# Score tiles in the outputs' PSUM banks, and three weight units split on VectorE, in a GLA and conformer step

## Chip, cores and metric

The kernel runs on one core of a Trainium2 chip, with float32 inputs and outputs. The metric is the device time of one execution in microseconds (us), taken as the median of several runs.

## The reference

One step of a two-layer streaming encoder. 512 new frames of one stream ("prompt") and 64 frames of a running one ("sample") pass through a gated-linear-attention (GLA) mixer and a conformer convolution mixer, each with a normalization ahead and a residual add. The change lies in the GLA mixer, whose core for one head is this:

```python
qe = qc * jnp.exp(b)                     # b: running sum of log decay
ke = kc * jnp.exp(-b)
att = jnp.where(mask, qe @ ke.T, 0.0)    # scores, causal
o = att @ vc + qe @ S                    # outputs; S is the state
S = jnp.exp(b_last) * S + (kc * jnp.exp(b_last - b)).T @ vc
...
o = o * lax.rsqrt(jnp.mean(o * o, axis=-1, keepdims=True) + EPS)
y = (o * g_norm * jax.nn.silu(r)) @ w_out
```

There are 4 heads with 256 key and 512 value features each. q, k, v and the gate r are columns of one projection `h @ w_in` with 2048 input features.

## The kernel before, in words

Activations lie feature-major: 128 features on the partitions, all 576 tokens as columns, and a PSUM bank takes half of them (288). Float32 precision comes from splitting each operand in a high and a low part; a projection is then three matmuls, high by high (L224), low activations by high weights (L227), high activations by low weights (L230).

Weights arrive in *units* of 8 blocks of 128 by 128 (512 KB). For a plain unit (`to_unit`, L118 to L131) SyncE's queue loads the raw values (L116, two buffers), ACT rounds them to the high part (L124), and the low part is made in one of two ways. Either DVE subtracts the high part from the raw values (L126), or, for units listed in `dma_lo`, ACT writes the negated raw values in the low part's format (L128) and a transfer issued by POOL adds the weights to it from DRAM (L129). The parts have four buffers.

The heads' stage (from L771) treats four heads, one after the other, with projection blocks of 128 columns laid between as *tiles* (`tile(i)`: two units, 96 matmuls, except the last, which holds three blocks). For each head:

- `decay(h)`: POOL issues loads of two small operands (a L775, w L776), TensorE multiplies them (pz L783), DVE and ACT turn the result into decays (L785 to L819, with scans at L795). `scores(h)` loads q and k from DRAM (ld L767) and scales them (L825).
- `attention(h)`: five score tiles `pa` (L847 to L860). Each has a product on the diagonal (L849), the first three also products with rescaled queries qs (L855, L859). `psum_split` copies each tile to a high part on ACT (athi L725) and a low part on DVE (atlo L726), and POOL masks them (L828). Then ACT scales the keys (kd L874) and TensorE transposes them (ptkd L732, pukd L735).
- `output(h)`: four output tiles po (L894) copied by ACT (o L896), and four small ones for the sample tokens pq (L899, L902) copied by DVE (o L903). Their squares are summed (L607, L610, L611).
- `states(h)`: the new states pS (L925), copied by ACT (so L933) or combined by DVE (s L928), and stored (sp L934, ss L930). `output(h)` loads the old sample state (s L885).
- `norm(h)`: the sums of squares are split (sso L465, L466), summed across partitions by TensorE (m_o L461), and turned into a factor on ACT and DVE (t_o L483, v_o L484, rs L485 to L488), which multiplies the outputs (L911).
- `gates(h)`, called inside the next head: the loaded gate multiplies the outputs (L943, on POOL for the first three heads), and they are spilled to DRAM (L945). The outputs have one buffer, so the next head's copy L896 waits for the last spill.

`values(h)` loads v by transfers that POOL issues (L959, L960). Results of the projection blocks are stored at L973.

PSUM has eight banks. Four belong to the projection (`ps`). Two carry the tag "ms": pz, the score tiles pa, the transposes, pq, pS and the norm's sums m_o take them in turn. Two carry the tag "main": the outputs po, and tiles of a later stage.

The order on each engine is set by a scheduler that simulates a time line, within the dependences and the program's order; `tile(2h + 2)` is bound to come behind the head's first score product, `tile(2h + 3)` behind its last transpose. An edit to a tag or a list so changes the order in places that the edit does not name.

Of the kernel before, what the change touches and what calls it, by code (L numbers as in the profile page):

```python
# [11 lines left out]
F32 = mybir.dt.float32  # L12
# [5 lines left out]
P = 128  # L18
# [31 lines left out]
def emit(nc, tc, x, wg, wa1, wa2, wgo, wc, wco, par, s0, y, sp_out, ss_out, cv_out):  # L50
# [30 lines left out]
    def psum_pool(key, name, bufs):  # L81
        psum[key] = tc.tile_pool(name=name, bufs=bufs, space=PSUM)
        return psum[key].__enter__()
# [6 lines left out]
    px = psum_pool("e", "pse", 1)  # L90
# [13 lines left out]
    def tmp(name, w=T, dt=F32):  # L104
        return s2.tile([P, w], dt, tag="s2", name=name)
# [3 lines left out]
    dma_lo = set()  # L109
# [158 lines left out]
    def plan(groups, srcf):  # L268
        for g in groups:
            for half in range(2):  # L270
                for b in g:
                    chunks.append(lambda i, w=srcf(b), half=half: plain_chunk(i, w, half))
# [241 lines left out]
    base_p = len(chunks)  # L514
    for i, (b, _) in enumerate(gla_pairs):
        plan_full(wg[b], wg[b + 1], ("ra", "rb")[i % 2])
    base_l = len(chunks)
    plan(gla_last, lambda b: wg[b])
    base_o = len(chunks)
# [3 lines left out]
    base_c = len(chunks)  # L523
    plan(conv_groups, lambda b: wc[b])
    base_co = len(chunks)
    dma_lo.update(range(4, base_p), range(base_l, base_o), range(base_c + 4, base_co))
    plan([[0, 1]], lambda f: wco[f])
    for f in range(2, 14, 2):
        plan_pair(wco[f], wco[f + 1])
# [194 lines left out]
    def psum_split(hi, lo, ps):  # L724
        nc.scalar.activation(hi, ps, AF.Copy)  # L725
        nc.vector.tensor_tensor(lo, ps, hi.bitcast(F32), ALU.subtract)  # L726

    def to_tok(src, dst, sample, name):

        pt = px.tile([P, 512], F32, tag="ms", bufs=2, name=f"pt{name}")  # L730
        for i in range(4):
            ins = nc.tensor.transpose(pt[:, i * P : (i + 1) * P], src[:, i * P : (i + 1) * P], ident).ins  # L732
        psum_split(dst[0], dst[1], pt.rearrange("p (i c) -> p i c", i=4))
        pt = px.tile([P, 512], F32, tag="ms", bufs=2, name=f"pu{name}")
        nc.tensor.transpose(pt[:TS, :P], src[:, TP:T], ident)  # L735
        psum_split(sample[0], sample[1], pt[:TS, :P])
        return ins
# [89 lines left out]
    def causal(ap, n):  # L827
        nc.gpsimd.affine_select(out=ap, in_=ap, compare_op=ALU.is_ge, fill=0.0, base=0,  # L828
                                pattern=[[1, n]], channel_multiplier=-1)
# [7 lines left out]
    def attention(h):  # L837

        d = hd[h]
        q, k = d["eq"], d["ek"]  # L840
        att = [gp.tile([P, 1344], F32R, tag=f"at{n}", name=f"at{n}{h}") for n in ("hi", "lo")]
        eo = 0
        first = None
        for i in range(5):
            n = TP - i * P if i < 4 else TS
            w = min(n, P)
            pa = px.tile([P, 512], F32, tag="ms", bufs=2, name=f"pa{h}_{i}")  # L847
            for dt in range(2):
                ins = nc.tensor.matmul(pa[:w, :w], k[:, dt, i * P : i * P + w], q[:, dt, i * P : i * P + w],  # L849
                                 start=(dt == 0), stop=(dt == 1)).ins  # L850
                first = first or ins
            if i < 3:
                for dt in range(2):
                    qs = tmp(f"qs{h}_{i}{dt}")
                    nc.vector.tensor_tensor(  # L855
                        qs[:, : n - P].rearrange("p (j t) -> p j t", t=P),
                        q[:, dt, (i + 1) * P : TP].rearrange("p (j t) -> p j t", t=P),
                        d["ee"][:, dt, eo : eo + 3 - i].unsqueeze(2).broadcast_to([P, 3 - i, P]), ALU.mult)
                    nc.tensor.matmul(pa[:, P:n], k[:, dt, i * P : (i + 1) * P], qs[:, : n - P],  # L859
                                     start=(dt == 0), stop=(dt == 1))  # L860
                eo += 3 - i
            o = OFFS[i]
            psum_split(att[0][:w, o : o + n], att[1][:w, o : o + n], pa[:w, :n])
            for t in att:
                causal(t[:w, o : o + w], w)
        d["qs"] = gp.tile([P, 2, TS], F32, tag="qs", name=f"qsm{h}")
        nc.vector.tensor_copy(d["qs"], q[:, :, TP:])
        d["att"] = att
        kd = [gp.tile([P, 5, DKH], F32R, tag=f"kd{n}", name=f"kd{n}{h}") for n in ("hi", "lo")]
        for dt in range(2):  # L870
            kt = tmp(f"kd{h}{dt}")
            for i in range(5):
                n = P if i < 4 else TS
                nc.scalar.activation(kt[:, i * P : i * P + n], k[:, dt, i * P : i * P + n], AF.Copy,  # L874
                                     scale=d["km"][:, dt, i : i + 1])
            js = slice(dt * P, (dt + 1) * P)
            ins = to_tok(kt, [t[:, :4, js] for t in kd], [t[:TS, 4, js] for t in kd], f"kd{h}{dt}")
        d["kd"] = kd
        return first, ins
# [104 lines left out]
    for h in range(H):  # L984
        scored, turned = attention(h)
        if h:
            gates(h - 1)
        if h < 3:
            start_head(h + 1)
        if h == 0:  # L990
            tile(1)
        tile(2 * h + 2, scored)
        output(h)
        if h < 3:
            scores(h + 1)
        states(h)
        norm(h)
        if h < 3:
            tile(2 * h + 3, turned)
            values(h + 1)  # L1000
# [271 lines left out]
def build():  # L1272
    nc = _bacc.Bacc("TRN2", target_bir_lowering=False, num_devices=1)

    def inp(name, shape):
        return nc.dram_tensor(name, shape, F32, kind="ExternalInput").ap()

    def out(name, shape):
        return nc.dram_tensor(name, shape, F32, kind="ExternalOutput").ap()

    args = [
        inp("x", [P, KT, T]),
        inp("wg", [48, P, KT, P]),
        inp("wa1", [P, KT, RANK]),
        inp("wa2", [96, 1024]),
        inp("wgo", [16, P, KT, P]),
        inp("wc", [48, P, KT, P]),
        inp("wco", [16, P, KT, P]),
        inp("par", [P, PC_N]),
        inp("s0", [P, 8, DVH]),  # L1290
        out("y", [P, KT, T]),
        out("sp", [P, 8, DVH]),
        out("ss", [P, 8, DVH]),
        out("cv", [P, 16, 2 * PAD]),
    ]
    with TileContext(nc, schedule_with_timeline_sim=True) as tc:
        emit(nc, tc, *args)
    return nc
# [47 lines left out]
```

## Time and profile before

| | us |
|---|---|
| median of 3 runs | 1771.37 (1769.4 to 1772.29) |
| the profiled execution | 1776.21 |
| its span in the trace | 1774.5 |

The mean granted TensorE clock of the profiled execution was 0.985 of full speed. The heads' stage lies at about 440 to 740 us of its span.

A row of a waits view tells the engine, what it computes and the line, behind the arrow what ended the wait, then the total in us, how often and the longest. Rows of a timeline tell the start, the duration, the engine, line and operation, output and inputs, their sizes and the count, and in brackets the idle time ahead and its end. PE is TensorE, PEld its weight load, DVE VectorE, ACT ScalarE, POOL GpSimd and SP SyncE.

### The profile page before, as it was taken

To read this page: it belongs to the slowest core of one execution; us is meant where nothing else is said; L and a number is where in the kernel's file an instruction comes from. 1 tells how busy PE (TensorE), PEld (TensorE's weight loads), DVE (VectorE), ACT (ScalarE), POOL (GpSimd) and SP (SyncE) were. 2 spreads that over 40 slices of the span, in tenths; PEclk is the share of its full clock that TensorE was granted. 3 is DMA by queue.
4 is the path that set the end of the run, shared out by engine and by line. 5 is a ranking of instruction groups with operands and counts; after the bars stand their busy time and mean duration, and the time that the engine had idled before them with its cause. 6 is when DMAs were issued, how large, how long until landed. Compare 5 with 4: busy or idle time off the path is not lost.

```text
span 1774.5 us, 31017 instructions
## 1 busy us (share of the span) xinstructions
PE 1722.7 (97%) x12606; PEld 1695.9 (96%) x12606; DVE 1126.0 (63%) x1622; ACT 906.9 (51%) x1229; POOL 491.8 (28%) x455
## 2 busy tenths in 40 slices
PE   8999999999999989999999999999999989999996
PEld 8999999999888878999999999999999989999995
DVE  7677777766344551845566889878888751185554
ACT  7653343345656563623246556565566574353433
POOL 3100000000222313022223455545555442133221
PEclk9999999999999999999999999999999999999998
DMA  7963455434966864643336777877778768623323
GB/s 236 246 154 120 135 148 149 135 122 132 271 178 195 252 188 140 214 135 128 129 130 164 165 163 166 169 162 164 165 160 180 171 151 171 149 74 118 111 89 133
DMA packets 108896, 282.15 MB, mean 159 GB/s; under 512 B 10672, under 2 KB 37168, under 8 KB 107728
## 3 DMA queue, kind: packets, MB, share of 16 engines
q1 hardware_dynamic: 87632, 202.33, 37.9%
q0 software_dynamic: 21120, 77.83, 22.3%
q8 instruction: 99, 1.62, 0.4%
q14 instruction: 45, 0.37, 0.1%
HBM read 242.68 MB, written 37.45 MB: 158 GB/s over the span
## 4 chain that ended last, share of the span: by engine, by line
PE 81%; DVE 6%; DMA 6%; ACT 3%; issue 2%; POOL 1%; SPq 0%; ACTq 0%; DVEq 0%; POOLq 0%
PE ps L230 14%; PE ps L224 14%; PE ps L227 14%; PE d L391 14%; PE c L337 9%; PE c L328 6%; PE db L391 2%; DMA wlo<-wg 2%; PE po L894 1%; DMA spill<-o 1%; PE cb L328 1%; DVE c L1181 1%; PE pS L925 1%; PE pq L337 1%; PE pq L444 1%
## 5 line engine op out<-in xcount | busy, mean ns | idle before, releaser
L124 ACT ACTIVATE whi<-raw 128x1024 fp32r<-128x1024 f32 x296 | 313.5, 1059 | 498.7 <-PE ps L227 160.3
L227 PE MATMUL ps<-h1l,whi 128*128 128x288 f32 x1536 | 330.1, 296 | 0.0
L230 PE MATMUL ps<-h1h,wlo 128*128 128x288 f32 x1536 | 329.7, 296 | 0.0
L224 PE MATMUL ps<-h1h,whi 128*128 128x288 f32 x1536 | 329.6, 296 | 0.0
L1118 DVE SCALAR_TENSOR_TENSOR acc<-ux,pr,acc 128x606 f32<-128x606 f32 x352 | 297.7, 852 | 11.8 <-ACT acc L1108 2.2
L126 DVE TENSOR_TENSOR wlo<-raw,whi 128x1024 fp32r<-128x1024 f32 x168 | 208.4, 1241 | 132.3 <-ACT whi L124 130.1
L224 PEld LDWEIGHTS ps<-h1h,whi 128*128 128x128 f32 x1536 | 248.5, 189 | 0.0
L227 PEld LDWEIGHTS ps<-h1l,whi 128*128 128x128 f32 x1536 | 248.5, 189 | 0.0
L230 PEld LDWEIGHTS ps<-h1h,wlo 128*128 128x128 f32 x1536 | 248.4, 189 | 0.0
L1116 POOL TENSOR_TENSOR sd<-sd,sd 128x606 f32<-128x606 f32 x96 | 153.5, 1599 | 73.4 <-ACT sd L1112 72.2
L129 POOL DMA_DIRECT2D wlo<-wg x36 | 31.8, 882 | 478.7 <-DVE tb L420 335.7
L611 POOL TENSOR_TENSOR ssq<-ssq,sq_x 128x576 f32<-128x576 f32 x35 | 64.0, 1829 | 286.9 <-ACT sq_x L610 281.4
L129 POOL DMA_DIRECT2D wlo<-wc x92 | 80.9, 880 | 218.0 <-ACT wlo L128 170.2
L128 ACT ACTIVATE wlo<-raw 128x1024 fp32r<-128x1024 f32 x128 | 133.6, 1044 | 0.1
L391 PE MATMUL d<-nh,whi 128*128 128x288 f32 x448 | 132.6, 296 | 0.0
L391 PE MATMUL d<-nh,wlo 128*128 128x288 f32 x448 | 131.9, 294 | 0.0
L391 PE MATMUL d<-nl,whi 128*128 128x288 f32 x448 | 131.8, 294 | 0.0
L1112 ACT ACTIVATE sd<-ux,pr 128x606 f32<-128x606 f32 x112 | 87.3, 793 | 55.8 <-POOL sd L1116 55.8
L230 PE MATMUL ps<-nh,wlo 128*128 128x288 f32 x480 | 108.4, 303 | 2.5 <-DMA wlo<-wg 2.5
L227 PE MATMUL ps<-nl,whi 128*128 128x288 f32 x480 | 107.1, 302 | 0.0
L224 PE MATMUL ps<-nh,whi 128*128 128x288 f32 x480 | 106.9, 302 | 0.0
L391 PE MATMUL d<-S,whi 128*128 128x288 f32 x448 | 90.3, 295 | 0.0
(542 smaller groups left out, 3877.8 us busy)
## 6 DMA issues: line engine op xcount, KB each, us to landing
raw<-wc SPq DMA_DIRECT2D x96, 512.0 KB, 4.8
raw<-wg SPq DMA_DIRECT2D x94, 512.0 KB, 4.7
wlo<-wc POOLq DMA_DIRECT2D x92, 512.0 KB, 7.6
wlo<-wg POOLq DMA_DIRECT2D x36, 512.0 KB, 8.6
raw<-wco SPq DMA_DIRECT2D x26, 512.0 KB, 3.8
raw<-wgo SPq DMA_DIRECT2D x25, 512.0 KB, 4.2
ld<-pd SPq DMA_DIRECT2D x29, 288.0 KB, 5.3
vd<-v SPq DMA_DIRECT2D x32, 256.0 KB, 4.6
```

Of the source, the lines that this page charges most:

```text
L124: nc.scalar.activation(hi[:, :w, :], raw, AF.Copy)
L126: nc.vector.tensor_tensor(lo[:, :w, :], raw, hi[:, :w, :].bitcast(F32), ALU.subtract)
L128: nc.scalar.activation(lo, raw, AF.Copy, scale=-1.0)
L129: nc.gpsimd.dma_start(lo, src, accum_op=ALU.add)
L224: nc.tensor.matmul(ps[j], hi[:, kk, :], ah[k][:, j * HT : (j + 1) * HT], start=st, stop=False)
L227: nc.tensor.matmul(ps[j], hi[:, kk, :], al[k][:, j * HT : (j + 1) * HT], start=False, stop=False)
L230: nc.tensor.matmul(ps[j], lo[:, kk, :], ah[k][:, j * HT : (j + 1) * HT], start=False, stop=sp)
L328: nc.tensor.matmul(dst, w[:, o + k, :], v, start=start and k == 0 and i == 0, stop=stop and k == 3 and i == 2, skip_group_check=True)
L337: nc.tensor.matmul(dst[j], w[:, k, :], v[:, j * HT : (j + 1) * HT], start=start[j] and k == 0 and i == 0, stop=stop[j] and k == 7 and i == ...
L391: nc.tensor.matmul(dst, w[:, k, :], v, start=first and k == 0 and i == 0, stop=k == 7 and i == 2, skip_group_check=True)
L1116: nc.gpsimd.tensor_tensor(side, side, t, ALU.add)
L1118: nc.vector.scalar_tensor_tensor(a, v3(u[:, w : w + CW]), cw(w), a, ALU.mult, ALU.add)
```

## The change

Two edits. The score tiles `pa` take their PSUM bank from the tag "main", in turn with the outputs po, and no longer from "ms", where the norm's sums stay. And the first three plain units of the heads' tiles (both of tile 0 and the first of tile 1) leave `dma_lo`, so that DVE makes their low parts by a subtraction (L126) in place of ACT's negated copy (L128) and POOL's adding transfer (L129). The computed values are the same.

```diff
-    dma_lo.update(range(4, base_p), range(base_l, base_o), range(base_c + 4, base_co))
+    dma_lo.update(range(4, base_p), range(base_l + 3, base_o), range(base_c + 4, base_co))
...
-            pa = px.tile([P, 512], F32, tag="ms", bufs=2, name=f"pa{h}_{i}")
+            pa = px.tile([P, 512], F32, tag="main", bufs=2, name=f"pa{h}_{i}")
```

## Prediction

> **What bounds the kernel now.** I read the page first, for what is left to win at all.
>
> ```profile
> span 1774.5 us, 31017 instructions
> PE 1722.7 (97%) x12606; PEld 1695.9 (96%) x12606; DVE 1126.0 (63%) x1622; ACT 906.9 (51%) x1229; POOL 491.8 (28%) x455
> ```
>
> TensorE is busy 97% of the span. An edit that takes no matmul away can win only its idle time, 1774.5 - 1722.7 = 51.8 us, and time in which it ran at a lower clock. The second view is the busy time by stretches of 60 us over the heads (columns: stretch, its us, busy PE, PEld, DVE, ACT, POOL, granted TensorE clock, share of the DMA engines, GB/s).
>
> ```profile
> 440.00:500.00 60.00, 56.14 (x408) 54.11 (x407) 18.36 (x49) 36.81 (x57) 15.02 (x28) 1.00 0.96 260
> 500.00:560.00 60.00, 55.81 (x364) 51.25 (x363) 29.55 (x62) 34.57 (x55) 19.60 (x27) 0.97 0.74 211
> 560.00:620.00 60.00, 55.95 (x348) 50.21 (x347) 30.20 (x64) 38.03 (x60) 19.58 (x27) 0.94 0.72 200
> 620.00:680.00 60.00, 53.32 (x326) 47.18 (x325) 28.93 (x61) 35.86 (x56) 17.47 (x24) 0.94 0.71 203
> ```
>
> The heads are where TensorE is not at its best: 3.9 to 6.7 us of each 60 idle, and a clock of 0.94 in two rows. Nothing else is near its limit, except that the DMA engines are at 0.96 in the first row. The third view is TensorE's waits there, 440 to 740 us (line that waits, what ended the wait, total, times, longest).
>
> ```profile
> PE pa L849 <- DVE v_o L484: 6.0, 3, 4.2
> PE po L894 <- ACT o L896: 4.2, 3, 1.8
> PE ps L230 <- DMA wlo<-wg: 2.5, 2, 1.3
> PE pS L925 <- ACT so L933: 1.8, 2, 1.2
> PE pz L783 <- DMA w<-w2d: 1.2, 1, 1.2
> PE m_o L461 <- ACT sso2h L465: 1.1, 1, 1.1
> PE m_o L461 <- ACT sso1h L465: 1.1, 1, 1.1
> PE pa L849 <- DVE atlo L726: 1.0, 1, 1.0
> PE pS L925 <- DVE o L903: 0.9, 2, 0.4
> PE m_o L461 <- DVE sso1l L466: 0.3, 1, 0.3
> PE m_o L461 <- DVE sso2l L466: 0.3, 1, 0.3
> ```
>
> They sum to 20.4 us. The first row is the one that the change speaks to: a head's first score product needs a bank of the tag "ms", both hold the last norm's sums, and v_o (L484) is their last reader. TensorE's timeline at the longest:
>
> ```profile
> 529.45 0.42 PE L461 MATMUL m_o<-sso0l,onesr 128*128 128x288 f32 x2
> 534.07 1.05 PE L849 MATMUL pa<-eq,c 128*128 128x128 f32 x4 [4.19 <-DVE v_o L484]
> ```
>
> Its price is more than 4.19 us. These are the stretches of the heads at half clock, and under them the 3.4 us ahead of three of them and two stretches that stayed at full clock:
>
> ```profile
> 534.30:537.70 3.40, 3.40 (x16) 3.40 (x16) 3.33 (x8) 1.60 (x2) 0.00 (x0) 0.50 1.10 381
> 592.30:599.10 6.80, 5.98 (x22) 5.53 (x23) 3.04 (x7) 2.64 (x4) 0.46 (x1) 0.50 1.01 299
> 653.80:660.60 6.80, 5.96 (x23) 5.42 (x24) 2.85 (x6) 3.08 (x5) 0.94 (x2) 0.50 1.02 286
> 687.90:694.70 6.80, 6.80 (x25) 6.13 (x24) 0.27 (x2) 1.96 (x3) 1.41 (x1) 0.50 0.07 15
> 588.90:592.30 3.40, 1.89 (x7) 0.94 (x7) 1.51 (x2) 3.34 (x6) 2.62 (x5) 1.00 0.66 156
> 650.40:653.80 3.40, 2.01 (x8) 0.96 (x7) 1.50 (x2) 3.38 (x6) 2.14 (x4) 0.99 0.47 134
> 684.50:687.90 3.40, 1.60 (x11) 1.46 (x12) 0.18 (x1) 1.09 (x2) 0.00 (x0) 1.00 0.98 237
> 619.60:623.00 3.40, 2.60 (x20) 2.37 (x18) 0.94 (x2) 0.00 (x0) 0.00 (x0) 1.00 0.97 250
> 623.00:626.40 3.40, 2.46 (x14) 2.26 (x15) 0.00 (x0) 1.39 (x3) 0.00 (x0) 1.00 0.95 262
> ```
>
> Stretches with TensorE busy 1.6 to 2.0 us of 3.4 were followed by half clock, those with 2.5 to 2.6 were not. Three of the four begin where a head's norm sums and first products wait. At 0.50 a stretch loses half its length: 3.4/2 + 3 x 6.8/2 = 11.9 us. So 20.4 + 11.9 = 32.3 us can be won in the heads, and no more.
>
> [...]
>
> **The change part by part.** *Score tiles in "main".* No instruction is added; the wait of L849 on v_o goes, and with it the reason for the order around it. TensorE's own order at the start of head 1 (ps: projection matmuls, m_o: norm sums of head 0, pa: scores of head 1), before:
>
> ```order
> L230 MATMUL ps_0_1_5648<-nh_1036,wlo_5355 128x288
> L461 MATMUL m_o_5629<-sso0h,onesr 128x288
> L461 MATMUL m_o_5634<-sso0h,onesr 128x288
> L461 MATMUL m_o_5629<-sso0l,onesr 128x288
> L461 MATMUL m_o_5634<-sso0l,onesr 128x288
> L849 MATMUL pa_0_5773<-eq_5187,c_1_5186 128x128 x2
> L224 MATMUL ps_0_0_5930<-nh_957,whi_5409 128x288
> ```
>
> And now:
>
> ```order
> L461 MATMUL m_o_5626<-sso0l,onesr 128x288
> L461 MATMUL m_o_5631<-sso0l,onesr 128x288
> L227 MATMUL ps_0_0_5644<-nl_1012,whi_5351 128x288
> ...
> L230 MATMUL ps_0_1_5645<-nh_1036,wlo_5352 128x288
> L849 MATMUL pa_0_5770<-eq_5184,c_1_5183 128x128 x2
> L859 MATMUL pa_0_5770<-qs_00_5773,c_1_5183 128x384
> ```
>
> Between the last norm sum and the first score 34 projection matmuls now stand, and 9 more among the sums; before there were none, because tile 3's were used up. At 56.14/408 = 0.138 us apiece (first 60 us row) they cover 4.7 us, more than the 4.19. In heads 2 and 3 first score products stand ahead of the last norm sums, with 20 to 40 projection matmuls around them, so the waits of m_o and of pa there have cover too. Gone by this: v_o 6.0, m_o 1.1 + 1.1 + 0.3 + 0.3 = 2.8, atlo 1.0: 9.8 us. Of the pS waits (1.8 + 0.9 = 2.7) I take 1.0, since the pS banks stay in "ms" but no score tile queues for them.
>
> The clock follows: the first three stretches go, 1.7 + 3.4 + 3.4 = 8.5 us. The fourth starts behind the po wait, which has another cause. The chain of waits there:
>
> ```profile
> 617.29 5.77 DMA spill<-o
> ...
> 652.77 12.17 DMA ss<-s
> 665.45 3.37 DMA ld<-pd
> ...
> 677.62 7.85 DMA spill<-o
> 685.64 0.61 ACT o L896
> ```
>
> The outputs have one buffer, so ACT's o (L896) waits for the last head's spill, and po behind it. The score tiles ending sooner do not move that by themselves: what moves it is the earlier gates. I take half of the po wait, 2.1 of 4.2, and half of the fourth stretch, 1.7 of 3.4; the bounds are none and all.
>
> *What the move adds.* po and pa now alternate in two banks: a po must wait for the split (L725, L726) of the fourth and fifth score tile, a score tile of the next head for the last po's copy. The copies of a head's po end before its norm sums can begin, which sum their squares, so the second costs nothing; for the first, the transposes of kd stand between. In head 0 the scheduler uses the freedom otherwise. TensorE's order at head 0's first transposes (ptkd), before:
>
> ```order
> L849 MATMUL pa_4_5137<-eq_4908,c_0_4907 64x64 x2
> L230 MATMUL ps_0_1_5351<-nh_996,wlo_5025 128x288
> L224 MATMUL ps_0_0_5350<-nh_1001,whi_5236 128x288
> L732 MATMUL ptkd_5154<-ident,kd_5148 128x128 x4
> L224 MATMUL ps_0_1_5351<-nh_1001,whi_5236 128x288
> ```
>
> And now:
>
> ```order
> L859 MATMUL pa_1_5101<-qs_11_5107,c_0_4904 128x256
> L230 MATMUL ps_0_1_5230<-nh_1021,wlo_4967 128x288
> ...
> L230 MATMUL ps_0_0_5229<-nh_1031,wlo_4967 128x288
> L732 MATMUL ptkd_5151<-ident,kd_5145 128x128
> L230 MATMUL ps_0_1_5230<-nh_1031,wlo_4967 128x288
> ```
>
> The transposes stand 12 projection matmuls (1.7 us) behind the second score tile, not behind the fifth. They need kd (L874), and ACT does kd behind a unit whose load is late:
>
> ```profile
> 478.75 1.06 ACT L124 ACTIVATE whi<-raw 128x1024 fp32r<-128x1024 f32 x1 [5.25 <-DMA raw<-wg]
> 480.66 1.50 ACT L874 ACTIVATE kd<-c,ke 128x128 f32<-128x128 f32 x5
> ```
>
> If the load is as late as here TensorE stands up to 5.25 us, if it comes sooner not at all; I take the middle, 2.6, and half of one 6.8 us stretch's loss, 1.7. In the last heads the scaled queries (L855) use buffers that the state copies free; a wait of 1.2 us, the longest of the pS row, is put in, between 0 and twice that.
>
> *Low parts on DVE.*
>
> ```profile
> L126 DVE TENSOR_TENSOR wlo<-raw,whi 128x1024 fp32r<-128x1024 f32 x168 | 208.4, 1241 | 132.3 <-ACT whi L124 130.1
> L129 POOL DMA_DIRECT2D wlo<-wg x36 | 31.8, 882 | 478.7 <-DVE tb L420 335.7
> L128 ACT ACTIVATE wlo<-raw 128x1024 fp32r<-128x1024 f32 x128 | 133.6, 1044 | 0.1
> ```
>
> DVE gains 3 x 1.241 = 3.7 us in a stretch where it is busy 18.36 of 60; ACT loses 3 x 1.044 = 3.1 us, POOL's queue 3 x 0.882 = 2.6 us, and three 512 KB loads leave a stretch in which the DMA engines are at 0.96. On the path this ends two waits: ps on wlo 2.5 and, since POOL issues the w load (L776) behind these, pz 1.2. Together 3.7. The cover of DVE's 3.7 us is the projection itself; without it the cost would be 3.7 once.
>
> *The sum.* Gone: 9.8 + 1.0 + 8.5 + 2.1 + 1.7 + 3.7 = 26.8. New: 2.6 + 1.7 + 1.2 = 5.5. Net 21.3 us. Behind the heads TensorE had no idle time that could swallow this:
>
> ```profile
> 760.00:820.00 60.00, 60.00 (x453) 60.00 (x452) 30.38 (x43) 19.59 (x24) 16.57 (x12) 1.00 0.43 144
> ```
>
> With 60.00 of 60 us busy there, a sooner start reaches the end. The profiled execution was 1776.21 us (span 1774.5 and 1.7 outside), so 1754.9; it lies 4.84 us above the median of the runs, 1771.37. Taken from the median: 1750.1. Bounds: with nothing new and all won 32.3, so 1739.1; with the po terms at nothing and the new ones at 5.25 + 3.4 + 2.4, 23.0 - 11.0 = 12.0, so 1759.4.
>
> **The rivals.** *The waits come back elsewhere, half clock with them.* [...] For it: transposes and po now queue closely. If only the first stretch goes and one new 6.8 us stretch comes: waits 9.8 + 3.7 = 13.5, clock 1.7, less 5.5 and 3.4: 6.3, so 1765.1.
>
> *Half clock stays.* If the three drops that follow no long idle time have a cause other than these waits, they stay: waits 9.8 + 1.0 + 2.1 + 3.7 = 16.6, clock 1.7, less 2.6 and 1.2: 14.5, so 1756.9. Against it: each begins right behind a window with waits in it. [...]
>
> *The spill chain is the bound.* Each head waits for the last one's spills; the three steps of the chain above, 12.17, 3.37 and 7.85 us, follow one another. If it sets the pace, what goes at pa comes back at po: no change, 1771. Against it: po's waits are 4.2 us in all, so it is at most near.
>
> *SyncE's queue (slower).* The order of its transfers at head 3, before (s: state, ld: queries and keys, raw: weights):
>
> ```order
> L885 DMA s_3_7158<-s 128x1024
> L767 DMA ld_7024<-pd 128x576
> ...
> L767 DMA ld_7036<-pd 128x576
> L945 DMA spill<-o_6630 128x576 x2
> L116 DMA raw_7389<-wg 128x1024
> L945 DMA spill<-o_6630 128x576 x2
> ```
>
> And now:
>
> ```order
> L885 DMA s_3_7155<-s 128x1024
> L116 DMA raw_7386<-wg 128x1024
> L767 DMA ld_7021<-pd 128x576
> ...
> L767 DMA ld_7033<-pd 128x576
> L973 DMA pd<-p_0_7149 128x288
> L945 DMA spill<-o_6627 128x576
> L973 DMA pd<-p_1_7152 128x288
> L116 DMA raw_7441<-wg 128x1024
> L945 DMA spill<-o_6627 128x576 x3
> ```
>
> Three spills now stand behind a weight load and two result stores. A weight load waits in the queue for its buffer:
>
> ```profile
> SPq L116 <- ACT wlo L128: 41.0, 4, 17.5
> ```
>
> If such a wait, up to 17.5 us, falls ahead of the spills, ACT's o and po wait for it, and half clock follows (3.4): 20.9 a head, in two heads 41.8 against 21.3 won, so 20.5 slower, 1791.9. It decides from 21.3/2 = 10.7 us a head. Against it: three of the four waits on that row are shorter, and ACT has less to do.
>
> **How the numbers follow.** About 0.2%, 3.5 us, is what a measurement of this kernel can tell from no change. Forecast (15 to 30 us won) 0.57; half clock stays (about 14) 0.06; waits that come back (4 to 14) 0.15; more than 30 won 0.07; no change 0.07; slower 0.08. The first four are faster: 0.85. The range takes the forecast and the first two rivals, 1740 to 1767, and leaves out about 0.2.
>
> **What would show it.** Right: no wait of L849 on v_o; ps on wlo gone before 500 us; at most two half-clock stretches in the heads, none at the norm sums; 60 us rows of the heads with 57 us busy or more. Wrong: po waiting on ACT's o for more than 4.2 us in all, ptkd waiting on kd for over 5 us, or the last spills issued later against their head's first po than now.

## The result and the profile after

| | us | ratio to before (95% interval) |
|---|---|---|
| before, median | 1771.83 (1768.37 to 1775.64) | |
| changed, median | 1752.31 (1750.50 to 1755.05) | 0.9891 (0.9874 to 0.9908) |
| changed, on another occasion | 1752.15 (1750.70 to 1756.74) | 0.9880 (0.9863 to 0.9897) |
| profiled execution, span before and changed | 1774.5 and 1753.3 | |

The changed kernel is 19.5 us faster; 21.3 was forecast, and the time lies in the range. One execution of a kernel tried below (changed, sums moved too) took 5518.86 us, and its ratio leaves that one out. The page of the changed kernel:

```profile
span 1753.3 us, 31000 instructions
PE 1713.8 (98%) x12606; PEld 1689.8 (96%) x12606; DVE 1126.7 (64%) x1625; ACT 903.3 (52%) x1226; POOL 488.4 (28%) x452
```

TensorE's waits in the changed kernel from 440 to 730 us, all of them:

```profile
PE pz L783 <- DMA w<-w2d: 2.6, 1, 2.6
PE pa L849 <- DVE qsm L867: 1.9, 1, 1.9
PE pS L925 <- DVE o L903: 1.3, 2, 0.7
PE pa L849 <- issue: 0.9, 1, 0.9
PE pq L899 <- DVE o L903: 0.8, 1, 0.8
PE po L894 <- POOL athi L828: 0.3, 1, 0.3
```

They sum to 7.8 us, against 20.6 before: the 20.4 of the named rows and 0.2 on "issue", which is idle time for which the profile shows no cause. L849 no longer waits for v_o, the sums no longer for their parts, ps no longer for wlo, and po no longer for ACT's copies. Two stretches at half clock are left (columns as before: stretch, us, busy PE, PEld, DVE, ACT, POOL, clock, DMA share, GB/s):

```profile
608.02:611.43 3.41, 3.41 (x17) 3.41 (x16) 0.91 (x2) 0.27 (x1) 0.00 (x0) 0.50 0.93 214
635.33:638.74 3.41, 3.41 (x11) 2.67 (x10) 0.00 (x0) 1.99 (x4) 0.87 (x1) 0.50 0.48 154
```

They start behind the two longest waits of the list, pz at 607.57 us and pa at 633.87. (The row of pa names the copy qsm; pa itself reads the queries and keys, which DVE scales just around that copy.) A second profile of the same kernel, with a span of 1750.5 us, has both waits again, 2.7 and 1.9 us, and 7.8 us in all, but half clock behind the first alone; so the second stretch, an estimated 1.7 us lost, need not come. The loss is estimated here as half of TensorE's busy time at half clock: equal products of pS (L925, 128x512) start 0.43 us apart inside the second stretch, at 636.14 and 636.57 us, and 0.22 us apart just behind it, at 638.96 and 639.18. The four stretches of before hold 3.41 + 6.03 + 5.99 + 6.83 = 22.3 us of work, so 11.1 lost, these two 6.8, so 3.4 lost:

```profile
534.29:537.70 3.41, 3.41 (x16) 3.41 (x16) 3.34 (x8) 1.61 (x2) 0.00 (x0) 0.50 1.09 380
592.32:599.15 6.83, 6.03 (x22) 5.53 (x23) 3.09 (x7) 2.62 (x4) 0.44 (x1) 0.50 1.01 300
653.76:660.59 6.83, 5.99 (x23) 5.46 (x24) 2.85 (x6) 3.12 (x5) 0.97 (x2) 0.50 1.02 289
687.89:694.72 6.83, 6.83 (x25) 6.16 (x24) 0.28 (x2) 1.96 (x3) 1.41 (x1) 0.50 0.07 15
```

Waits 20.6 - 7.8 = 12.8 us and clock 11.1 - 3.4 = 7.7 make 20.5 of the 21.2 us between the two spans. The same in stretches of 60 us:

```profile
440.00:500.00 60.00, 59.10 (x433) 57.45 (x432) 27.86 (x73) 40.44 (x61) 12.02 (x23) 1.00 0.86 235
500.00:560.00 60.00, 60.00 (x404) 55.59 (x403) 25.06 (x50) 38.59 (x62) 20.46 (x28) 1.00 0.80 238
560.00:620.00 60.00, 56.82 (x369) 52.11 (x369) 27.98 (x62) 36.83 (x58) 20.12 (x28) 0.97 0.74 212
620.00:680.00 60.00, 56.23 (x360) 50.36 (x359) 28.01 (x61) 35.09 (x60) 21.03 (x27) 0.97 0.66 195
```

TensorE is busy 56.82 and 56.23 us in the last two rows; the prediction had named 57 or more as a sign of being right, so this sign holds in two rows of four.

One thing in the trace is not what it seems. ACT's copies of the outputs wait *longer* for the spills than before, though TensorE does not (the waits view of ACT, changed kernel, 440 to 740 us; before it said 10.1 us in 3 waits):

```profile
ACT o L896 <- DMA spill<-o: 20.5, 3, 10.3
```

The heads reach that point sooner and projection matmuls are left to do meanwhile. The spill chain is still there, covered.

### The profile page after: what moved, and what is told of

It reads as the page before. It is cut to its first block, busy times and chain, and to the rows that moved or that the text cites. A ratio compares the mean times of both kernels' runs of the same rounds, so it can differ in the third digit from the quotient of the medians.

```text
span 1753.3 us, 31000 instructions
## 1 busy us (share of the span) xinstructions
PE 1713.8 (98%) x12606; PEld 1689.8 (96%) x12606; DVE 1126.7 (64%) x1625; ACT 903.3 (52%) x1226; POOL 488.4 (28%) x452
## 4 chain that ended last, share of the span: by engine, by line
PE 86%; DVE 6%; DMA 3%; ACT 3%; issue 1%; POOL 1%; SPq 0%; DVEq 0%; ACTq 0%; POOLq 0%
PE d L391 15%; PE ps L227 15%; PE ps L224 15%; PE ps L230 15%; PE c L337 9%; PE c L328 6%; PE db L391 3%; PE pS L925 2%; PE cb L328 1%; PE po L894 1%; DVE c L1181 1%; DMA raw<-wg 1%; PE pq L337 1%; PE pq L444 1%; DVE x L1242 1%
## 5 line engine op out<-in xcount | busy, mean ns | idle before, releaser
L126 DVE TENSOR_TENSOR wlo<-raw,whi 128x1024 fp32r<-128x1024 f32 x171 | 212.0, 1240 | 134.7 <-ACT whi L124 132.5
L129 POOL DMA_DIRECT2D wlo<-wc x92 | 81.1, 881 | 219.1 <-ACT wlo L128 167.4
L128 ACT ACTIVATE wlo<-raw 128x1024 fp32r<-128x1024 f32 x125 | 130.5, 1044 | 0.0
```

The costliest lines, as they stand in the source:

```text
L126: nc.vector.tensor_tensor(lo[:, :w, :], raw, hi[:, :w, :].bitcast(F32), ALU.subtract)
L128: nc.scalar.activation(lo, raw, AF.Copy, scale=-1.0)
```

## The experiments

A kernel's gain is 1772 us times one minus its ratio to the kernel before, run on the same chip. Each median is of 4 to 12 executions, so the intervals differ in width.

| kernel | median us | ratio (95% interval) | gain us |
|---|---|---|---|
| bank only | 1765.08 | 0.9950 (0.9931 to 0.9969) | 8.9 |
| low parts only | 1775.26 | 0.9999 (0.9984 to 1.0015) | 0.2 |
| sums moved, scores not | 1767.93 | 0.9968 (0.9954 to 0.9983) | 5.7 |
| changed, sums moved too | 1765.12 | 0.9939 (0.9917 to 0.9961) | 10.8 |
| bank only, early loads | 1763.48 | 0.9949 (0.9929 to 0.9970) | 9.0 |
| changed, early loads | 1757.55 | 0.9911 (0.9882 to 0.9940) | 15.8 |
| changed, six units on DVE | 1759.76 | 0.9924 (0.9900 to 0.9949) | 13.5 |
| changed, one unit on DVE | 1759.75 | 0.9929 (0.9906 to 0.9953) | 12.6 |
| changed, spills by quarters | 1755.59 | 0.9892 (0.9877 to 0.9907) | 19.1 |
| changed, early loads, spills by quarters | 1747.16 | 0.9850 (0.9835 to 0.9865) | 26.6 |
| before, spills by quarters | 1767.49 | 0.9963 (0.9949 to 0.9977) | 6.6 |

**Bank only.** The kernel before with this edit:

```diff
-            pa = px.tile([P, 512], F32, tag="ms", bufs=2, name=f"pa{h}_{i}")
+            pa = px.tile([P, 512], F32, tag="main", bufs=2, name=f"pa{h}_{i}")
```

> Only the score tiles' bank is moved; the low parts stay on ACT and POOL's transfers. Theory (the wait of the next head's scores for the readers of the norm's sums, with the half clock behind it, is most of the gain; DVE's low parts are worth the 3.7 us of the forecast): 17.6 us under before, about 1754, no wait of L849 on v_o, at most two half-clock stretches in the heads, and ps on wlo (2.5 us) still there. Rival (the two edits work only together, since the low parts place the projection matmuls that cover the sums: this order has 27, 17 and 35 projection matmuls between the last sum and the scores, the changed kernel 34, 37 and 31): under half of the gain, 1762 or more, with waits at head 2, where 17 matmuls cover only 2.3 us.

It gained 8.9 us, half of what the theory gave. The wait on v_o is gone, as it had said; its largest waits from 440 to 745 us show what came:

```profile
PE pz L783 <- DMA w<-w2d: 5.4, 2, 4.3
PE pS L925 <- DVE o L903: 4.0, 2, 3.3
PE ps L230 <- DMA wlo<-wg: 2.7, 2, 1.4
PE po L894 <- ACT o L896: 2.2, 2, 1.5
```

pz, po and pS each have half clock behind or around them:

```profile
551.59:558.42 6.83, 5.97 (x20) 5.42 (x21) 0.94 (x2) 3.54 (x5) 2.05 (x4) 0.50 0.92 228
623.27:626.68 3.41, 3.41 (x14) 3.12 (x13) 0.00 (x0) 3.38 (x3) 0.00 (x0) 0.50 0.19 71
633.51:640.34 6.83, 5.34 (x13) 4.20 (x14) 6.57 (x22) 5.29 (x8) 2.87 (x2) 0.50 0.09 33
```

So the rival that the edits work only together holds for the size, though not for its reason: the loss is not at the sums, where few matmuls stand, but at other waits, pz in head 1 and po and pS in head 2.

**Low parts only.**

```diff
-    dma_lo.update(range(4, base_p), range(base_l, base_o), range(base_c + 4, base_co))
+    dma_lo.update(range(4, base_p), range(base_l + 3, base_o), range(base_c + 4, base_co))
```

> Only the three units' low parts are moved to DVE; the score tiles stay with the norm's sums. Theory: 3.7 us under before, about 1768; the waits of ps on wlo and of pz on w before 500 us are gone, L849 still waits for v_o in heads 2 and 3, where nothing stands between the sums and the scores, and their half-clock stretches stay. Rival (the low parts are what moves the order, and 10 projection matmuls now stand between sums and scores at head 1): the 4.19 us wait there shrinks by 10 x 0.138 = 1.4 us or goes whole with its half clock, so up to 5.9 us more, about 1762.

It gained nothing that can be measured, and both theories fall. The waits at the start are gone (ps on wlo, pz on w), but the time is given back at the sums of heads 1 and 2. Its waits, and one of them in TensorE's timeline:

```profile
PE m_o L461 <- ACT sso1h L465: 8.6, 1, 8.6
PE m_o L461 <- ACT sso2h L465: 8.6, 1, 8.6
PE po L894 <- ACT o L896: 4.1, 2, 2.3
PE pa L849 <- DVE v_o L484: 1.7, 2, 0.8
```

```profile
591.88 0.85 PE L461 MATMUL m_o<-sso1h,onesr 128*128 128x288 f32 x2 [8.57 <-ACT sso1h L465]
```

In the kernel before the same sum starts at 590.79 us, after a wait of 1.1. TensorE came there some 6 us earlier and stood, because ACT was behind: ahead of the split of the squares (sso1h), which ends the wait, it did the next head's decays, a weight unit and a copy of the state. Where sums and scores share banks, the first score comes behind the sums, and the next tile is bound behind the first score, so TensorE had no matmuls left to do meanwhile; what was won ahead of the sums was lost at them in this run.

**The sums moved, the scores not.** The kernel before with this edit:

```diff
-                m = pool_s[0].tile([P, 512], F32, tag="ms", bufs=2, name=f"m_{name}{j}")
+                m = pool_s[0].tile([P, 512], F32, tag="main" if name[0] == "o" else "ms", bufs=2, name=f"m_{name}{j}")
```

> The other way round: the heads' norm sums go to the outputs' banks and the score tiles stay in the tag of before; low parts as before. Theory (it is the sharing of one pair of banks by sums and scores that costs, whichever of the two leaves): as with the bank alone, 15 to 18 us under before, 1754 to 1757, no wait of L849 on v_o. Rival (the gain is that the score tiles make room in their old tag for the transposes and the states' products, which also use it): under 6 us, 1766 or more, with waits of ptkd, pq or pS in place of those on v_o.

A gain of 5.7 us (3.0 to 8.2), with no wait on v_o. That is below the 15 to 18 of the theory and what the rival gave, under 6, and the waits that the rival named came too: pS waits 6.9 us in all and ptkd 1.1. So the room that the score tiles leave in their old tag counts as well. The interval overlaps that of the bank alone (5.5 to 12.2): to part the two is worth something whichever leaves, but not the forecast's sum.

**The changed kernel, with the sums moved too** (the same edit, on the changed kernel).

> The changed kernel, with the heads' norm sums put in the scores' new banks as well, so that sums and scores share a pair of banks again while the old tag stays relieved. Theory (the sharing costs): the four sums stand right ahead of the scores again in heads 2 and 3, L849 waits for v_o there (about 0.95 + 0.84 us), the sums for their parts (2.8 us) and two half-clock stretches come back (6.8 us): about 11 us above the changed kernel, 1763. In head 1 34 projection matmuls stay between, and nothing comes back there. Rival (room in the old tag is the gain): within 3 us of the changed kernel, 1752.

It is 8.5 us slower than the changed kernel by the ratios (10.8 against 19.3), 11 were expected: the sharing itself costs, and room in the old tag is not the whole gain. The wait is back at the two heads where the sums stand ahead of the scores, and at head 1, where 34 matmuls stand between, it is not:

```profile
591.56 1.22 PE L849 MATMUL pa<-eq,c 128*128 128x128 f32 x4 [5.62 <-DVE v_o L484]
```

```profile
652.46 1.22 PE L849 MATMUL pa<-eq,c 128*128 128x128 f32 x4 [5.62 <-DVE v_o L484]
```

The price had other parts than expected: 5.6 us twice for v_o, not 0.9, and nothing at the sums themselves. Not all of it is the sharing: L849 also waited 3.0 us on "issue" at head 0, where no sums stand ahead, with 3.41 us at half clock behind it (0.9 and none in the changed kernel).

**Early loads, on the bank alone and on the changed kernel.** POOL's loads of a and w move out of `decay(h)` into `decay_loads(h)` and are issued ahead of the gates (the hunks that split the function are left out):

```diff
         scored, turned = attention(h)
+        if h < 3:
+            decay_loads(h + 1)
         if h:
             gates(h - 1)
```

> The bank alone, as in the run before, with one more edit: POOL issues the loads of the decays' two operands (a and w) ahead of the last head's gates and no longer behind the first of them. The bank alone was 8.8 us under before, 10.5 short of the changed kernel; 8.0 of that lies at 540 to 600 us, where pz waits 4.3 us for w behind a gate and half clock follows (6.8 us at half, 3.4 lost). Theory (the low parts helped there only by letting the gates come sooner): the early loads win the same 7.7 us, about 16.5 under before. Rival (what is lost at head 2 is where the projection matmuls lie): 9 us under before, plus or minus 3, with the idle time at pS or at the sums.

> The changed kernel with the same early loads of a and w. Its longest wait is pz on w, 2.6 us at 607 us, with one half-clock stretch of 3.4 us behind it (1.7 lost). Theory: both go, 4.3 us under the changed kernel, about 23.5 under before. Rival (the decays come sooner but the next wait, the sums on their parts on ACT as with the low parts alone, takes it all): within 2 us of the changed kernel.

Why these: in the changed kernel POOL's timeline has the loads behind three gates, and pz waits for them at 607.57.

```profile
595.22 1.43 POOL L943 TENSOR_TENSOR o<-o,ld 128x576 f32<-128x576 f32 x1 [1.68 <-DMA s<-s]
...
597.21 3.15 POOL L943 TENSOR_TENSOR o<-o,ld 128x576 f32<-128x576 f32 x2
599.97 0.86 POOL L775 DMA_DIRECT2D a<-a3d  x1
600.53 0.83 POOL L776 DMA_DIRECT2D w<-w2d  x1
```

Neither gained: 9.0 against 8.9 for the bank alone, 15.8 (10.6 to 20.9) against 19.3. The wait that they aim at is gone in both (on the bank alone one of 1.9 us stays at head 0, whose loads did not move), and others came. On the bank alone those are pS on the small outputs' copies, 3.9 us, and po on ACT's, 2.8. On the changed kernel it is these, in a profile of 1761.13 us, near the slow end of six executions from 1749.98 to 1762.10. Around the wait of po stand 10.24 us at half clock:

```profile
PE pS L929 <- DVE o L907: 4.3, 2, 2.3
PE po L898 <- ACT o L900: 3.8, 1, 3.8
PE pa L853 <- issue: 1.4, 1, 1.4
```

```profile
669.24:679.48 10.24, 9.40 (x34) 8.65 (x34) 0.58 (x3) 3.97 (x7) 2.81 (x2) 0.50 0.12 43
```

(Lines of the kernels with early loads stand four higher from L783 on: L898 is po, L900 its copy.)

**One unit or six on DVE**: `base_l + 1` and `base_l + 6` in the change's list.

> The changed kernel with one unit's low part on DVE in place of three. Theory (each of the units' own waits counts): one of the two waits of ps on wlo comes back, 1.2 us, and the second unit's transfer still collides: 1 to 4 us slower than the changed kernel. Rival (the low parts count by the order that they bring): its order at head 2 has the sums ahead of the scores with 2 projection matmuls between, against none ahead of a first score in the changed kernel, so it falls back to the bank alone, about 10 us slower.

> The changed kernel with six units' low parts on DVE in place of three. Theory (the first three matter because their transfers collide at the start of the heads, later ones do not): within 3.5 us of the changed kernel. Rival (it is ACT's time, 1.04 us a unit, and POOL's queue that matter): 3 to 6 us faster than it. Its order has 14 projection matmuls between the sums and the scores of head 2, so a third outcome, slower by several us, would say that the order decides.

Both gain about 6 us less than the changed kernel, with intervals that overlap its own a little (8.3 to 16.7 for one and 9.0 to 17.7 for six, against 16.3 to 22.3). With one unit, pz waits 3.5 us, ps on wlo 2.1; that lies between the theory, 1 to 4 us slower, and the rival, about 10. With six, pS waits 3.7 at head 1 and po 3.4 at head 3. Neither theory foresaw six to be slower. The third outcome named for it, that the order decides, fits, though the waits are not at the sums and scores of head 2 that it named: three units looks less like a point on a slope than like one order among several.

**The spills by quarters.** One tile serves the outputs of all heads, so the first copy waits for the spill of its quarter and not for all four (the line that makes the empty list `oall` is left out):

```diff
-        ob = big.tile([P, 4, T], F32, tag="big", name=f"o{h}")
+        ob = oall[0] if oall else oall.append(big.tile([P, 4, T], F32, tag="big", name="o")) or oall[0]
```

It was tried on the kernel before, on the changed kernel and on the changed kernel with the early loads, beside the changed kernel once more.

> The same tile for all heads in the kernel before, with nothing else changed: the price of the spill chain there. Theory (it is a wait of its own, 4.2 us with one half-clock stretch of 6.8 us, 3.4 lost): 5 to 7 us under before. Rival (the sums hold the next head back in any case): within 2 us of before, the time going to the waits of the sums and of L849 on v_o.

> The changed kernel with one tile for the outputs of all heads, in place of a new one from the same single buffer for each: the first copy of a head's outputs then waits for the spill of its own quarter and not for all four. In the changed kernel ACT's copies wait 20.5 us for spills, TensorE's po not at all. Theory (the spill chain is covered by projection matmuls there and costs nothing): within 3 us of the changed kernel. Rival (the chain still sets the pace of a head, through the copies and the squares behind them): 4 to 8 us faster than it.

> The same tile for all heads, in the changed kernel with the early loads of a and w. There the wait of pz went and po on ACT's copy came, 3.8 us with 10.2 us at half clock behind it (5.1 lost). Theory (that wait is the spills' and took the gain of the early loads): it goes, 8 us faster than with the early loads alone, 3 to 5 us faster than the changed kernel. Rival (another wait, pS on the copies of the small outputs, takes its place): within 2 us of the changed kernel or slower.

> The changed kernel itself once more, for its time beside the others of this set: 16 to 22 us under before.

The sizes came out near the theories. On the kernel before it gains 6.6 us (5 to 7 expected): the po waits on ACT's copies are gone, those on v_o stay at 6.1. The way there was another in part: in the profiles all waits fell by 2.2 us only, since others grew, and the clock's estimated loss from 11.1 to 3.2, because besides the stretch behind po that of head 2's sums is gone and head 1's is half as long, with the same waits ahead of them. On the changed kernel it gains nothing (1755.59 against 1752.15, 3.4 us slower, or 2.2 by the ratios; within 3 was expected): ACT's wait for spills falls from 21.7 us to 2.3, but TensorE did not stand for it, and one wait of pS on ACT's copy of the state, 5.6 us, came. With the early loads it takes away the wait that had eaten their gain: 1747.16, 5.0 us below the changed kernel run beside it (1746.49 to 1749.93, against 1750.70 to 1756.74). This is the fastest version. It has no half clock in the heads (the granted clock is 1.00 in each stretch of 60 us from 440 to 680 us) and these waits, 3.9 us in all:

```profile
PE pS L929 <- DVE o L907: 3.0, 2, 2.1
PE pa L853 <- issue: 0.9, 1, 0.9
```

## Why the prediction was right, and where it was not

- **Waits at the sums and scores (9.8 us).** All gone in the changed kernel, and those on v_o are back, 11.2 us, when sums and scores share banks again. For v_o it is shown in both directions; the waits of the sums themselves did not come back in that run.
- **Half clock behind them (8.5).** The three stretches are gone. They held 15.4 us of work, so the term was 7.7 and not 8.5: the two of 6.83 us had 0.80 and 0.84 us without work in them, which the estimate counts as no loss. Part of it is chance: in the kernel before with spills by quarters, with the same waits at the sums of heads 1 and 2, one of these stretches came at half its length, 3.41 us, and one not at all.
- **po waits and the fourth stretch (half of each, 2.1 and 1.7).** Too low: 0.3 us of po waits is left, none of it on ACT's copies (0.5 in the second profile), and the stretch is gone. The reason given, earlier gates, does not show against the heads' own pace: in heads 2 and 3 the last spill is issued 6.0 and 5.0 us behind the head's first po, against 3.1 and 0.3 before. The prediction had named that as a sign of being wrong; it came true and cost TensorE nothing, because projection matmuls cover it. The spills by quarters on the changed kernel, which gained nothing, show the same.
- **Waits at the start (3.7).** ps on wlo is gone, and so is the pz wait there; another pz wait, 2.6 us, came at a later head. The forecast had the load of w behind the units' transfers on POOL's queue, and overlooked that it also stands behind the gates.
- **What is new (5.5).** The transposes of head 0, 2.6 + 1.7, cost nothing. The load came 1.73 us late and not 5.25, and kd was ready in time:

```profile
470.96 1.06 ACT L124 ACTIVATE whi<-raw 128x1024 fp32r<-128x1024 f32 x1 [1.73 <-DMA raw<-wg]
472.88 1.50 ACT L874 ACTIVATE kd<-c,ke 128x128 f32<-128x128 f32 x5
```

 The 1.2 us for the scaled queries did not come either: no wait on qs is in the list. In their place came pz 2.6, pa on qsm 1.9, "issue" 0.9, pq 0.8 and two half-clock stretches, 3.4: 9.6 us, as the first rival had it (short waits, half clock with them), in other places. So the net was near by luck, because errors of both signs met: the po terms too small by some 3.5, the new ones by 4.1, and the clock too large by 0.8. (pS, put at 1.0, fell by 1.4.)
- **The step that failed** is the one that adds the two edits up: 17.6 us for the bank and 3.7 for the low parts, each from its own waits. The runs gave 8.9, 0.2 and together 19.3 to 21.3, so the sum came out though its parts did not. A wait on TensorE ends a race of several chains (gates and loads on POOL, copies and parts on ACT, spills), and a row says which came last, not how far behind the next was.
- **SyncE's queue (the slower rival)** did not decide: the waits of weight loads until ACT has read their buffer are shorter than before (the row below, 25.2 us against 41.0, besides one new wait of 8.8 on ACT's ke), and the last spills hold up ACT's copies but not TensorE.

```profile
SPq L116 <- ACT wlo L128: 25.2, 4, 10.2
```

What stays open: why exactly three units bring the good order. The runs with one and six speak against the count of subtractions or transfers as the cause, since both gain less; no kernel was run with the changed kernel's order and the low parts of before.

## What to carry to other kernels

Price a wait together with the next one behind it: of three that lie close (banks shared by sums and scores, a load queued behind gates, a buffer freed all at once), taking one away gave 8.9 us (banks) or 6.6 (buffer), taking banks and load gave no more than banks alone (9.0 against 8.9), and all three with the low parts gave 26.6. Look for a barrier that holds back independent work, such as a bank that makes the next tile wait for the last norm: what is won ahead of it can be lost at it, as with the low parts alone. And where a scheduler sets the order, a neighbouring value of a constant can cost a third of what the edit gains (some 6 of 19 us here), so test two or three.

## What the runs showed of the hardware

In the heads of the changed kernel the granted clock was 0.50 for 3.41 us behind a wait of 2.58 us (pz) and again for 3.41 us behind one of 1.87 us (pa), and TensorE had also worked in the 3.41 us ahead of each, for 0.83 and 1.54 us. So a short wait can cost nearly three times itself: in the kernel before, 1.80 us of po had 6.83 us of work at half clock behind it, an estimated 3.4 lost. It need not. The kernel with 3.9 us of waits in the heads, none over 2.1, had no such stretch there, and the pa wait of the changed kernel had one in one profile and none in the other.

The length of the wait does not part the two: 1.80 (po) and 1.87 us (pa) had half clock behind them, 2.1 (pS in the fastest version) and 1.9 (pa in the second profile) had none. What does was not shown, and a forecast can count half clock behind a wait of this length only as a chance.
